# Expert weights in 4 MB loads with 32 KB rows, in a one-core encoder layer with sixteen experts

## The chip, the core and the metric

The kernel runs on one core of one Trainium2 chip. TensorE (PE in the profile) multiplies, VectorE (DVE), ScalarE (ACT) and GpSimd (POOL) do the element work, and sixteen DMA engines move data between HBM and the on-chip memory. SyncE (SP) computes nothing here: its queue issues nearly all loads. The metric is device time in microseconds of one launch. The kernel before took 1243.34 us (median of 3 runs, 1241.81 to 1243.98).

## The reference

```
h   = rmsnorm(x, g_pre_mix) * (1 + scale_m) + shift_m     # x: 512 tokens x 1024
mix = concat(retention(h), dilated_attention(h)) @ w_out
x   = x + gate_m * rmsnorm(mix, g_post_mix)
h   = rmsnorm(x, g_pre_ffn) * (1 + scale_f) + shift_f
aff = softmax(h @ w_router)                               # 16 experts
gates, idx = top_k(aff.T, 64)                             # every expert takes 64 tokens
for e in range(16):
    a = h[idx[e]] @ w_gate[e]                             # (64 x 1024) @ (1024 x 2048)
    u = h[idx[e]] @ w_up[e]
    y = (silu(a) * u) @ w_down[e]                         # (64 x 2048) @ (2048 x 1024)
    moe[idx[e]] += gates[e] * y
x   = x + gate_f * rmsnorm(moe, g_post_ffn)
```

All is float32. Each expert has three weight matrices of 8 MB, so the sixteen experts read 402.7 MB.

## The kernel before

The mixer takes the first 325 us or so and isn't changed but for small things. Then the experts follow one after the other (the loop `for pr in range(E // 2)` takes them in pairs).

**One expert.** `gate_up` computes both first products. The contraction over the 1024 inputs is cut in eight chunks of 128 (K chunks); `chunk_up` takes two of them at a time, loads 256 rows of `w_gate` and 256 of `w_up` (2 MB each), and issues for each weight tile 16 matmuls (L1057): the stationary operand is a 128x64 piece of the gathered tokens (`xeT`), the moving operand 128x512 of weights. Two matmuls stand side by side in the two column halves of the array (`tile_position`, the index `g`). After the eight K chunks the element work and eight transposes (L1074) follow, and `down` (L1099) does the last product with four loads of 512 rows of `w_down` (2 MB each). So an expert consumes twelve 2 MB loads, each with 16 matmuls.

**Rows and K order.** A load gives partition p adjacent rows of the matrix: two rows of 8 KB of `w_gate` or `w_up` (rows 2p and 2p+1 of the 256), four rows of 4 KB of `w_down`. That is 16 KB of adjacent memory per partition. Which input belongs to K chunk k follows from this; `ffn_chunk` (with a step of 2) takes the same inputs out of x for the router's transposes and for the gather.

**Where the weights lie.** Nine tiles of 2 MB are used in turn (`order`): two of `ring_b`, two of `ring_w[0]`, two of `ring_w[1]`, two of `ring_h`, one of `ring_c`. `ring_w` and `ring_h` hold the mixer's split operands before. `wtile` takes the next one and issues its load on SP. SP works in order: a load waits until the matmuls that read the tile's old content are done, and all loads behind it wait too. For the last pair of experts one tile leaves the ring (`own_tile`) and holds rows for the end.

**Work between the matmuls.** PE's order is written out with `pin`. Even experts carry the scatter of the pair before (L1112) between the matmuls of `gate_up`. Odd experts carry the gather for the next pair (L1021: stationary operand a K chunk of x, moving operand a selection matrix) after `gate_up` and between the matmuls of `down`. The last pair carries more: the last selection, sums of rows (L986).

**The end.** After the last expert's `gate_up` the first 512 rows of the result are written by four stores (`out<-w`, L1189, on SP), and at last an indirect store (L1199, on POOL) writes the last expert's 64 tokens over them. It waits for those four stores and for the last row of element work (L1198).

Of the kernel before, what the change touches and what calls it, by code (L numbers as in the profile page):

```python
# [46 lines left out]
def layer(ctx, tc, x, c, w_ada, b_ada, g_pre_mix, g_post_mix, g_pre_ffn, g_post_ffn,  # L47
# [68 lines left out]
    ring_h = pool(ctx, "ring_h", N_R, side="right")  # L116
    hparts_of = [ring_h.tile([P, 2, 4, S], F32R, name="w") for _ in range(2)]
    hhi = [hparts_of[k // 4][:, 0, k % 4] for k in range(KC)]
    hlo = [hparts_of[k // 4][:, 1, k % 4] for k in range(KC)]
# [795 lines left out]
    order = [ring_b] * N_B + [ring_w[0]] * N_R + [ring_w[1]] * N_R + [ring_h] * N_R + [ring_c] * N_C  # L915

    def wtile(shape, src=None):
        t = order[state["n"] % len(order)].tile(shape, F32, name="w")
# [1 line left out]
        if src is not None:  # L920
            nc.sync.dma_start(t, src)
        return t

    def own_tile(shape):

        i = state["n"] % len(order)
        order[:] = order[i:] + order[:i]
        state["n"] = 0
        return order.pop(0).tile(shape, F32, name="w")
# [305 lines left out]
```

## Time and profile before

| what | value |
|---|---|
| median of 3 runs | 1243.34 us |
| the profiled execution's own time | 1243.3 us |
| its span in the trace | 1241.6 us |
| PE busy | 1148.5 us (92%) |
| DVE, ACT, POOL busy | 372.0, 235.5, 83.7 us |
| moved by DMA | 456.02 MB, mean 367 GB/s |
| granted TensorE clock, mean | 0.993 of full |

The span is the trace's first to last event; the execution's own time is 1.7 us longer. Times in rows are microseconds from the span's start. A busy PE is not PE at its peak: matmuls are pipelined, and one that waits for the engine counts as busy.

### The profile page before, as it was taken

How to read it: one execution, taken by the hardware profiler on the slowest of the kernel's cores; microseconds unless marked ns; L12 is line 12 of the kernel's file. 1: busy time of each engine (PE TensorE's matmuls, PEld its weight loads, DVE VectorE, ACT ScalarE, POOL GpSimd, SP SyncE). 2: the span in 40 equal slices, each digit the busy share in tenths (PEclk: the TensorE clock that was granted, in tenths of full speed). 3: DMA queues.
4: the chain of work that ended last, by engine and by line, in shares of the span. 5: the costliest groups of instructions: out<-in, count | busy, mean ns of one | idle time of the engine just before them, and what ended most of it. 6: DMA issues, size and time to landing. Idle time of an engine off the chain costs nothing.

```text
span 1241.6 us, 14130 instructions
## 1 busy us (share of the span) xinstructions
PE 1148.5 (92%) x5756; PEld 546.6 (44%) x5757; DVE 372.0 (30%) x914; ACT 235.5 (19%) x479; POOL 83.7 (7%) x135
## 2 busy tenths in 40 slices
PE   8999999999999999999799879978997898789997
PEld 5777776776443433433243224323332433243332
DVE  4589878666410120121022101200210121012022
ACT  4765335344010100101010101001000100010110
POOL 1622022201000000000000000000000000000012
PEclk8999999999999999999999999999999999999998
DMA  9946745296989999999999999999999999999997
GB/s 292 271 136 196 228 149 146 78 362 252 394 348 427 428 426 427 427 428 425 428 429 425 428 428 427 428 427 427 428 426 428 426 429 426 427 428 427 427 428 309
DMA packets 80520, 456.02 MB, mean 367 GB/s; under 512 B 6180, under 2 KB 41352, under 8 KB 55496
## 3 DMA queue, kind: packets, MB, share of 16 engines
q1 hardware_dynamic: 79384, 450.63, 89.8%
q0 software_dynamic: 656, 2.36, 0.5%
q10 hardware_dynamic: 416, 2.14, 0.4%
q8 instruction: 45, 0.74, 0.2%
q14 instruction: 19, 0.16, 0.0%
HBM read 452.75 MB, written 2.36 MB: 367 GB/s over the span
## 4 chain that ended last, share of the span: by engine, by line
PE 52%; DMA 36%; issue 4%; DVE 4%; ACT 1%; POOL 1%; POOLq 0%; DVEq 0%; SPq 0%; ACTq 0%
PE gu L1057 18%; DMA w<-in_w_up_e 15%; DMA w<-in_w_down_e 15%; PE yb L1099 12%; PE tb L1021 5%; DMA w<-in_w_gate_e 3%; PE pj L104 2%; PE pj L105 2%; PE pj L106 2%; PE sb L1112 2%; DMA wa<-in_w_ada 1%; PE tb L1074 1%; PE at L463 1%; DMA out<-w 1%; PE at L452 1%
## 5 line engine op out<-in xcount | busy, mean ns | idle before, releaser
L1057 PE MATMUL gu<-w,xeT 128*64 128x512 f32 x2032 | 465.9, 600 | 50.9 <-DMA w<-in_w_gate_e 26.2
L1057 PEld LDWEIGHTS gu<-w,xeT 128*64 128x64 f32 x2032 | 135.7, 137 | 336.2 <-issue 244.7
L1099 PE MATMUL yb<-w,wide_h 128*64 128x512 f32 x1024 | 230.0, 596 | 10.5 <-DMA w<-in_w_down_e 10.1
L1099 PEld LDWEIGHTS yb<-w,wide_h 128*64 128x64 f32 x1024 | 70.3, 137 | 144.7 <-issue 126.3
L1071 DVE SCALAR_TENSOR_TENSOR wide_h<-gu,gcol,wide_h 128x512 f32<-128x512 f32 x32 | 24.0, 751 | 294.7 <-PE gu L1057 229.6
L1070 ACT ACTIVATE wide_h<-gu 128x512 f32<-128x512 f32 x32 | 19.1, 597 | 465.1 <-PE gu L1057 413.4
L1127 DVE TENSOR_TENSOR wide_y<-yb,wide_y 64x512 fp32r<-64x512 f32 x30 | 20.7, 689 | 200.0 <-ACT wide_y L1126 200.0
L1021 PE MATMUL tb<-sel,yx 128*128 128x128 f32 x512 | 68.1, 286 | 5.4 <-ACT wide_h L1075 4.7
L1116 DVE TENSOR_TENSOR w<-w,sb 128x512 f32<-128x512 f32 x56 | 38.5, 687 | 112.8 <-PE sb L1112 112.8
L1021 PEld LDWEIGHTS tb<-sel,yx 128*128 128x128 f32 x512 | 62.8, 197 | 21.0 <-ACT xeT L1025 11.4
L1175 POOL TENSOR_TENSOR w<-ident 128x64 f32<-128x64 f32 x2 | 0.6, 318 | 815.6 <-PE gu L1057 815.6
L1126 ACT CAST wide_y<-yb 64x512 fp32r<-64x512 f32 x30 | 17.4, 580 | 186.8 <-PE yb L1099 175.6
L104 PE MATMUL pj<-w,hi 128*128 128x512 f32 x112 | 47.1, 421 | 0.0
L1112 PE MATMUL sb<-wide_y,selT 128*128 128x512 f32 (+1 forms) x128 | 47.1, 448 | 0.0
L318 DVE SCALAR_TENSOR_TENSOR acc<-wa,sc,acc 128x512 f32<-128x512 f32 x56 | 44.4, 792 | 2.8 <-DMA wa<-in_w_ada 2.4
L106 PE MATMUL pj<-w,lo 128*128 128x512 f32 x112 | 44.5, 398 | 0.0
L105 PE MATMUL pj<-w,hi 128*128 128x512 f32 x112 | 44.5, 398 | 0.0
L1027 DVE TENSOR_SCALAR xeT<-tb,mod 128x128 f32<-128x128 f32 x32 | 13.1, 410 | 98.1 <-PE tb L1021 98.1
L1112 PEld LDWEIGHTS sb<-wide_y,selT 128*128 128x128 f32 (+1 forms) x128 | 19.0, 187 | 51.9 <-issue 51.9
L110 DVE TENSOR_TENSOR lo<-w,hi 128x512 fp32r<-128x512 f32 (+1 forms) x52 | 34.9, 674 | 16.0 <-ACT hi L109 11.7
L109 ACT CAST hi<-w 128x512 fp32r<-128x512 f32 (+1 forms) x52 | 30.2, 585 | 49.9 <-PE pj L105 32.1
L442 POOL TENSOR_SCALAR w<-w,rden 128x512 f32<-128x512 f32 x32 | 32.2, 1014 | 110.2 <-DVE rden L441 94.1
(296 smaller groups left out, 1125.4 us busy)
## 6 DMA issues: line engine op xcount, KB each, us to landing
w<-in_w_up_e SPq DMA_DIRECT2D x64, 2048.0 KB, 37.6
w<-in_w_gate_e SPq DMA_DIRECT2D x63, 2048.0 KB
w<-in_w_down_e SPq DMA_DIRECT2D x61, 2048.0 KB, 36.9
wa<-in_w_ada SPq DMA_DIRECT2D x32, 512.0 KB, 4.7
w<-in_w_ada SPq DMA_DIRECT2D x16, 512.0 KB, 7.3
w<-in_w_in SPq DMA_DIRECT2D x14, 512.0 KB, 5.1
w<-in_w_down_e SPq DMA_DIRECT2D x5, 1024.0 KB
w<-in_w_out SPq DMA_DIRECT2D x4, 1024.0 KB
```

Of the source, the lines that this page charges most:

```text
L104: nc.tensor.matmul(o, lhsT=l[0], rhs=r[0], start=start, stop=False)
L105: nc.tensor.matmul(o, lhsT=l[0], rhs=r[1], start=False, stop=False)
L106: nc.tensor.matmul(o, lhsT=l[1], rhs=r[0], start=False, stop=stop)
L109: nc.scalar.copy(hi, src)
L110: nc.vector.tensor_tensor(lo, src, hi, ALU.subtract)
L318: nc.vector.scalar_tensor_tensor(acc, w[:, k], sc[:, 2 * i + k:2 * i + k + 1], acc, ALU.mult, ALU.add)
L442: nc.gpsimd.tensor_scalar(p, p, rden[:, i:i + 1], 1.0, ALU.mult, ALU.mult)
L1021: pin(nc.tensor.matmul(tp[:, j], lhsT=ffn_chunk(x1[:, t], k), rhs=sel[:, t].rearrange("p e c -> p (e c)"), start=(t == 0 and j == 0), stop ...
L1057: pin(nc.tensor.matmul(gu[m][i][64 * g:64 * g + 64], lhsT=xe[:, k], rhs=w[q][:, f:f + 512], start=(k == 0), stop=(k == KC - 1), tile_posit ...
L1099: pin(nc.tensor.matmul(yb[64 * n:64 * n + 64], lhsT=hc(fc), rhs=ws[k][:, 512 * n:512 * n + 512], start=(fc == 0 and seeded is None), stop= ...
L1112: pin(nc.tensor.matmul(sb, lhsT=selT[u, P * t:P * t + P], rhs=y[u, f], start=(i == 0), stop=(i == 1)))
L1116: nc.vector.tensor_tensor(acc_at(t, f), acc_at(t, f), sb, ALU.add)
```

## The change

- From the third expert on the weights come in loads of 4 MB. A partition gets four adjacent rows of `w_gate` or `w_up`, or eight of `w_down`: 32 KB.
- The tiles of the ring are taken as pairs: `ring_b`, `ring_w[0]`, `ring_w[1]`, `ring_h` give four pairs. Three pairs lie side by side in memory and take one 4 MB load each; in the pair `ring_w[0]` the tiles stay apart, and what falls on it comes as two loads of 2 MB. The ninth tile (`own`) leaves the ring with the third expert.
- The first two experts, the last expert's second half of `gate_up` and its `down` keep loads of 2 MB and less. These too follow the new row order.
- The order within `gate_up` becomes: four K chunks of gate, four of up, four of gate, four of up. The step of `ffn_chunk` becomes 4.
- The hidden columns are dealt out otherwise, since partition p now holds rows 8p to 8p+7 of `w_down`: the two matmuls that stand side by side take the even and the odd columns of the weights. Their moving operand is read with a step of two elements (8 bytes) where it was contiguous.
- `wo_parts` and `hparts_of` become one tile each, so that a pair of slots can be taken over as one.

The core of the diff:

```diff
     def ffn_chunk(a, k):
-        return a[..., 256 * (k // 2) + k % 2:256 * (k // 2) + 256:2]
+        return a[..., 512 * (k // 4) + k % 4:512 * (k // 4) + 512:4]
...
-    order = [ring_b] * N_B + [ring_w[0]] * N_R + [ring_w[1]] * N_R + [ring_h] * N_R + [ring_c] * N_C
...
+    pairs = [ring_b, None, *[r.tile([P, 2, 4096], F32, name="w") for r in (ring_w[1], ring_h)]]
+    order = [r if r is None else r[:, i] for r in pairs for i in range(2)] + [own]
...
+    def pair_of(src, rows):
+        n = state["n"] % len(order)
+        if pairs[n // 2] is None:
+            r = rows // 2
+            return [w for h in range(2) for w in units_of(src[:, r * h:r * h + r], r)]
+        state["n"] += 2
+        u = pairs[n // 2].rearrange("p i (s f) -> p (i s) f", s=rows // 2)
+        nc.sync.dma_start(u, src)
+        return [u[:, s] for s in range(rows)]
...
     def rows_up(ex, j):
-        return [wsrc[ex, 256 * j:256 * j + 256].rearrange("(p s) f -> p s f", s=2) for wsrc in (w_gate, w_up)]
+        return [wsrc[ex, 512 * j:512 * j + 512].rearrange("(p s) f -> p s f", s=4) for wsrc in (w_gate, w_up)]
...
-                    f = 1024 * i + 512 * g
-                    pin(nc.tensor.matmul(gu[m][i][64 * g:64 * g + 64], lhsT=xe[:, k], rhs=w[q][:, f:f + 512],
+                    pin(nc.tensor.matmul(gu[m][i][64 * g:64 * g + 64], lhsT=xe[:, k], rhs=w[q][:, 1024 * i + g:1024 * i + 1024:2],
...
     def down_rows(ex, j):
-        return w_down[ex, 512 * j:512 * j + 512].rearrange("(p s) n -> p s n", s=4)
+        return w_down[ex, 1024 * j:1024 * j + 1024].rearrange("(p s) n -> p s n", s=8)
```

Three places of the instruction order. First SP's queue where the third expert's loads begin, before (`w_` and a number is a tile, the brackets say for which engines and DMA lanes the load waits):

```order
139 L921 DMA w_3729<-in_w_gate_e 128x4096 [waits DMAHW2_49,PE_49]
140 L921 DMA w_3731<-in_w_up_e 128x4096 [waits DMAHW3_49,PE_49]
141 L921 DMA w_3757<-in_w_gate_e 128x4096 [waits DMAHW4_49,PE_49]
142 L921 DMA w_3759<-in_w_up_e 128x4096 [waits DMAHW5_49,PE_49]
143 L921 DMA w_3793<-in_w_gate_e 128x4096 [waits DMAHW6_49,PE_49]
144 L921 DMA w_3795<-in_w_up_e 128x4096 [waits DMAHW7_49,PE_49]
145 L921 DMA w_3839<-in_w_gate_e 128x4096 [waits DMAHW0_49,PE_49]
```

and the same place after the change (`w_3293` is the pair of `ring_w[1]`, `w_3294` that of `ring_h`):

```order
139 L941 DMA w_3293<-in_w_gate_e 128x8192 [waits DMAHW2_49,PE_49]
140 L941 DMA w_3294<-in_w_up_e 128x8192 [waits DMAHW4_49,DMAHW3_49,PE_49]
141 L941 DMA ring_b_2763<-in_w_gate_e 128x8192 [waits DMAHW7_49,DMAHW6_49,PE_49]
142 L930 DMA w_3818<-in_w_up_e 128x4096 [waits DMAHW5_49,DMAHW0_49,PE_49]
143 L930 DMA w_3820<-in_w_up_e 128x4096 [waits DMAHW1_49,PE_49]
```

These five loads bring the whole of the expert's `gate_up`, for which eight loads stood (seven are shown). A load into a pair waits for the matmuls of both tiles' old contents. The fifth load of before went to the ninth tile; now the third load goes on to `ring_b`.

Second the first loads into the mixer's old tiles, before and then after:

```order
119 L921 DMA w_3365<-in_w_gate_e 128x4096 [waits PE_49]
120 L921 DMA w_3367<-in_w_up_e 128x4096 [waits PE_49]
121 L921 DMA w_3405<-in_w_gate_e 128x4096 [waits PE_49]
122 L921 DMA w_3407<-in_w_up_e 128x4096 [waits PE_49]
123 L921 DMA w_3436<-in_w_up_e 128x4096 [waits DMAHW0_49]
```

```order
119 L930 DMA w_3367<-in_w_gate_e 128x4096 [waits PE_49]
120 L930 DMA w_3386<-in_w_up_e 128x4096 [waits PE_49]
121 L930 DMA w_3293<-in_w_gate_e 128x4096 [waits PE_49]
122 L930 DMA w_3293<-in_w_up_e 128x4096
123 L930 DMA w_3294<-in_w_up_e 128x4096 [waits DMAHW0_49]
```

Rows 121 and 122 went to two tiles, each with its own wait for PE; now they are the halves of one tile, and the first of them has the only wait.

Third PE's queue in the third expert's `gate_up`, the first matmuls, before and then after (`gu` is the product in PSUM, `sb` the scatter):

```order
1467 L1057 MATMUL gu_3725<-w,xeT 64x512 [waits DMAHW2_49]
1468 L1057 MATMUL gu_3725<-w,xeT 64x512
1469 L1057 MATMUL gu_3726<-w,xeT 64x512 x2
1470 L1057 MATMUL gu_3725<-w,xeT 64x512 x2
1471 L1057 MATMUL gu_3726<-w,xeT 64x512 x2
1472 L1057 MATMUL gu_3727<-w,xeT 64x512 [waits DMAHW3_49]
```

```order
1468 L1086 MATMUL gu_3713<-w,xeT 64x512 [waits DMAHW2_49]
1469 L1086 MATMUL gu_3713<-w,xeT 64x512
1470 L1086 MATMUL gu_3714<-w,xeT 64x512 x2
1471 L1086 MATMUL gu_3713<-w,xeT 64x512 x2
1472 L1086 MATMUL gu_3714<-w,xeT 64x512 x2
1473 L1086 MATMUL gu_3713<-w,xeT 64x512 x2
1474 L1086 MATMUL gu_3714<-w,xeT 64x512 x2
1475 L1142 MATMUL sb<-wide_y,selT 128x512 [waits Activation_49]
1476 L1142 MATMUL sb<-wide_y,selT 128x512 [waits DVE_49]
```

One row stands for a side-by-side pair or two. The wait for the next load came after 16 matmuls of 2 MB and now comes after 32 of 4 MB.

## Rows read from the trace of the kernel before

**Rows 1.** The page: GB/s in 40 equal slices of the span.

```profile
GB/s 292 271 136 196 228 149 146 78 362 252 394 348 427 428 426 427 427 428 425 428 429 425 428 428 427 428 427 427 428 426 428 426 429 426 427 428 427 427 428 309
```

**Rows 2.** Two pairs of experts: stretch, busy by engine, clock, DMA share, GB/s.

```profile
425.00:528.00 103.00, 101.76 (x494) 40.00 (x492) 16.64 (x40) 9.27 (x17) 0.00 (x0) 1.00 1.01 427
620.00:738.00 118.00, 105.35 (x498) 39.71 (x494) 16.61 (x40) 9.87 (x18) 0.00 (x0) 1.00 1.01 427
```

**Rows 3.** PE in order of time, end of the fourteenth expert's `gate_up`: start, duration, [idle before].

```profile
1088.45 3.65 PE L1057 MATMUL gu<-w,xeT 128*64 128x512 f32 x16 [1.25 <-DMA w<-in_w_gate_e]
1093.34 3.65 PE L1057 MATMUL gu<-w,xeT 128*64 128x512 f32 x16 [1.24 <-DMA w<-in_w_up_e]
...
1153.20 3.65 PE L1057 MATMUL gu<-w,xeT 128*64 128x512 f32 x16 [0.30 <-DMA w<-in_w_up_e]
```

**Rows 4.** Weight loads of PE in order of time, last expert's `down`.

```profile
1228.55 0.14 PEld L1099 LDWEIGHTS yb<-w,wide_h 128*64 128x64 f32 x2 [0.29 <-issue]
1229.27 0.28 PEld L1099 LDWEIGHTS yb<-w,wide_h 128*64 128x64 f32 x4 [0.58 <-DMA w<-in_w_down_e]
...
1231.80 0.32 PEld L1099 LDWEIGHTS yb<-w,wide_h 128*64 128x64 f32 x4 [0.54 <-DMA w<-in_w_down_e]
```

**Rows 5.** DVE's last instruction; then the last store in the chain of waits.

```profile
1235.19 0.75 DVE L1198 SCALAR_TENSOR_TENSOR w<-w,sf 128x512 f32<-128x512 f32 x1 [0.66 <-POOL sf L1197]
...
1224.33 12.35 DMA out<-w
```

**Rows 6.** DMA queue q1 in three stretches (600:1200, 1226:1231, 3:8): packets, MB, share.

```profile
DMA packets 17593, 256.27 MB, mean 427 GB/s; under 512 B 1950, under 2 KB 1950, under 8 KB 1950
q1 hardware_dynamic: 17569, 255.91, 100.4%
...
DMA packets 467, 1.88 MB, mean 377 GB/s; under 512 B 54, under 2 KB 54, under 8 KB 420
q1 hardware_dynamic: 467, 1.88, 92.4%
...
q1 hardware_dynamic: 491, 1.82, 96.0%
```

**Rows 7.** SP's queue in order of time, loads of the first three experts.

```profile
297.19 0.33 SPq L921 DMA_DIRECT2D w<-in_w_gate_e  x1
303.02 0.81 SPq L921 DMA_DIRECT2D w<-in_w_up_e  x2
...
370.35 0.33 SPq L921 DMA_DIRECT2D w<-in_w_gate_e  x1
...
401.25 0.33 SPq L921 DMA_DIRECT2D w<-in_w_up_e  x1
...
422.02 0.33 SPq L921 DMA_DIRECT2D w<-in_w_gate_e  x1
```

**Rows 8.** DMA share (last but one) and GB/s; then tenths busy in 40 slices of 294:299.

```profile
368.00:371.00 3.00, 3.00 (x17) 1.00 (x14) 0.00 (x0) 0.00 (x0) 0.00 (x0) 1.00 0.15 60
...
DMA  9988420010000000000000000000000009930356
```

**Rows 9.** Groups of PE (count, busy us, mean ns, idle before) and of its weight loads.

```profile
L1057 PE MATMUL gu<-w,xeT 128*64 128x512 f32 x2032 | 465.9, 600 | 50.9 <-DMA w<-in_w_gate_e 26.2 <-DMA w<-in_w_up_e 24.2 <-DVE xeT L1027 0.5
...
L1099 PE MATMUL yb<-w,wide_h 128*64 128x512 f32 x1024 | 230.0, 596 | 10.5 <-DMA w<-in_w_down_e 10.1
...
L1021 PEld LDWEIGHTS tb<-sel,yx 128*128 128x128 f32 x512 | 62.8, 197 | 21.0 <-ACT xeT L1025 11.4 <-ACT wide_h L1075 6.1 <-issue 2.4
L1074 PEld LDWEIGHTS tb<-ident,wide_h 128*128 128x128 f32 x128 | 17.9, 208 | 20.3 <-DVE wide_h L1071 14.1 <-ACT wide_h L1075 6.2
L1112 PEld LDWEIGHTS sb<-wide_y,selT 128*128 128x128 f32 x112 | 16.7, 188 | 45.4 <-issue 45.4
...
L807 PEld LDWEIGHTS at<-ident,yx 128*128 128x128 f32 x32 | 4.6, 207 | 2.8 <-issue 1.6 <-PE m L106 0.9
L950 PEld LDWEIGHTS tb<-ident,sel 128*128 128x128 f32 x32 | 3.8, 144 | 0.0
```

More of the change, by code (lines that the diff above doesn't have):

```diff
@@ L115, in layer @@
     sm = pool(cm, "sm", 4)
[L116 to L119, printed above, removed]
+    ring_h = pool(ctx, "ring_h", side="right")
+    hparts_of = ring_h.tile([P, 2, 2, 4, S], F32R, name="w")
+    hhi = [hparts_of[:, k // 4, 0, k % 4] for k in range(KC)]
+    hlo = [hparts_of[:, k // 4, 1, k % 4] for k in range(KC)]
     wsp = pool(cq, "wsp", 2, side="right")
@@ L684, in layer @@
     cq.close()
-    ring_w = [pool(ctx, f"ring_w{n}", N_R, side="right") for n in range(2)]
+    ring_w = [pool(ctx, f"ring_w{n}", 2 - n, side="right") for n in range(2)]
+    wo_parts = ring_w[1].tile([P, 2, 2, 4, 512], F32R, name="w")
     KS = [4, 5, 6, 7, 0, 1, 2, 3]
@@ L696, in wo_split @@
         yield
-        parts = ring_w[n].tile([P, 2, 4, 512], F32R, name="w")
+        parts = wo_parts[:, i] if n else ring_w[0].tile([P, 2, 4, 512], F32R, name="w")
         hi, lo = parts[:, 0], parts[:, 1]
@@ L910, in layer @@
     mw = pool(ctx, "mw", 1)
-    ring_c = pool(ctx, "ring_c", N_C)
+    own = pool(ctx, "own").tile([P, 4096], F32, name="own")
     psg = pool(ctx, "psg", 1, space=PSUM)
@@ L914, in layer, with unit, units_of, large @@
     state = {"n": 0}
[L915 to L918 removed]
+    pairs = [ring_b, None, *[r.tile([P, 2, 4096], F32, name="w") for r in (ring_w[1], ring_h)]]
+    order = [r if r is None else r[:, i] for r in pairs for i in range(2)] + [own]
+    def unit():
         state["n"] += 1
[L920 to L929, printed above, removed]
+        o = order[(state["n"] - 1) % len(order)]
+        return ring_w[0].tile([P, 4096], F32, name="w") if o is None else o
+    def units_of(src, rows, cut=None):
+        u = unit().rearrange("p (s f) -> p s f", s=rows)
+        for s0, m in cut or ((0, rows),):
+            nc.sync.dma_start(u[:, s0:s0 + m], src[:, s0:s0 + m])
+        return [u[:, s] for s in range(rows)]
[7 more added lines that the diff above has]
+        nc.sync.dma_start(u, src)
+        return [u[:, s] for s in range(rows)]
+    def large(ex, late):
+        if ex < WHOLE:
+            return False
+        if len(order) % 2:
+            while state["n"] % len(order) % 2:
+                state["n"] += 1
+            if state["n"] % len(order) == len(order) - 1:
+                state["n"] += 1
+            state["n"] %= len(order)
+            order.pop()
+        return ex < E - 1 or not late
     def acc_tiles():
@@ new lines, in down @@
+        for j in range(2):
+            src = down_rows(ex, j)
+            whole = large(ex, True)
+            if whole:
+                ws = pair_of(src, 8)
+            for h in range(2):
+                if whole:
+                    w = ws[4 * h:4 * h + 4]
+                elif first and (j, h) == (0, 0):
+                    w = [first[s // 2][:, s % 2] for s in range(4)]
+                else:
+                    w = units_of(src[:, 4 * h:4 * h + 4], 4, None if ex < E - 1 or j == 0 else ((0, 2), (2, 1), (3, 1)) if h else ((0, 2), (2, 2)))
+                for s in range(4):
+                    fc = 8 * j + 4 * h + s
+                    for n in range(2):
+                        pin(nc.tensor.matmul(yb[64 * n:64 * n + 64], lhsT=hc(fc), rhs=w[s][:, 512 * n:512 * n + 512],
+                           start=(fc == 0 and seeded is None), stop=(fc == 15), tile_position=(0, 64 * n)))
+                    if s % 2:
+                        next(side, None)
@@ L1143, in layer @@
         sels = pair_sel(es, gcol)
-        if last:
-            own = own_tile([P, 4096])
         if pr == 0:
```

69 lines of the change are left out of this document (28 added, 41 removed).

## Prediction

> **What bounds the kernel now.** I read the GB/s line of the page first. From the thirteenth slice (372 us) to the last but one it stands at 425 to 429 [rows 1]: the stream of weights never pauses there. Then two pairs of experts by stretch. Between 425 and 528 us a pair takes 103 us with PE busy all along; between 620 and 738 us it takes 118 us, PE is busy for 105, DMA for all of it [rows 2]. So PE starts behind a full ring, empties it, and from about 570 us waits for weights. In such a stretch a burst of 16 matmuls starts at each landing, 4.89 us apart (1088.45, 1093.34), works 3.65 us and waits 1.25 [rows 3]. A load of 2.097 MB in 4.9 us is the 427 GB/s again.
>
> The end is less plain. The wait at 1093.34 (the fourteenth expert's last weights) is PE's last long one: the scatter, the last selection and the sums of rows then keep it busy, and up to 1233 us it waits for weights only 0.30 us at 1153.20 [rows 3] and twice in the last `down`, 0.58 and 0.54 where 0.29 is usual between weight loads, so 0.29 and 0.25 [rows 4]. From 1093 us on PE's own work and the stream are level. The last row of element work is ready at 1235.19 + 0.75 = 1235.94; the last plain store lands at 1224.33 + 12.35 = 1236.68 and releases the indirect store [rows 5]. The stream wins by 0.7 us. A change must therefore be followed on two paths: the stream, and PE from the fourteenth expert's last weights on.
>
> **Part 1: longer rows (gain).** Does a longer packet cost less per byte? Between 600 and 1200 us queue q1 moved 17569 packets, 1950 of them under 512 B; the other 15619 share 255.91 MB, 16 KB each [rows 6]. The engines' time is 1.004 x 16 x 600 us, or 617.1 ns a packet. At 1226 to 1231 us there are 366 packets of 4 KB and 47 of 8 KB (467 less 54 small ones; 420 under 8 KB) in 0.924 x 16 x 5 = 73.9 us [rows 6]. If a packet costs a + b per KB, then a + 16b = 617.1 and 413a + 1840b = 73920, hence a = 9.9 ns. The stretch 3 to 8 us gives another end: 1.82 MB of 4 KB packets in 0.960 x 80 us are 173 ns each [rows 6], hence a = 25 ns; those loads start into an empty queue, so I take 10, the row on the saturated queue. No row shows a packet above 16 KB. If it stays cut at 16 KB the gain is nothing; that is the other end of the range.
>
> A 4 MB load has 128 rows, 8 per engine; each saves one a, 80 ns per load. The order has 60 such loads: 80 pairs of 2 MB from the third expert to the last one's first half, less the quarter that falls on `ring_w[0]`. All 60 make 4.8 us. Up to the fourteenth expert's last weights, and after the gap below, there are 51: -4.1 us.
>
> **Part 2: a pair must be free as a whole (loss, once).** While PE leads, a load leaves when PE frees its tile. The load at 370.35 finds the stream empty (DMA share 0.15 between 368 and 371) [rows 7, 8]; bytes follow an issue by about 0.9 us (issue at 297.19; the DMA line of 294 to 299 fills at its 34th of 40 slices, 298.1) [rows 7, 8]. So the stream restarts at about 371.2. Ten loads leave between 370.35 and 401.25, 49.0 us of work at 4.9: it lasts to 420.2. Before, two more loads had left by then. Now the third 4 MB load needs both tiles of `ring_b`, and the second of these is freed at 422.02 [rows 7]; its bytes come at 423.0. The gap is 423.0 - 420.2 = 2.8 us; since the restart is only known to half a us, I take +2.5. All weights behind it are that much later. The first loads into `ring_w[1]` leave at 303.02 instead of 297.19 [rows 7], since both halves of `wo_parts` must be read out. That lateness of 5.8 us meets the idle 368 to 371.2 and, what is left, the gap just counted; it isn't added. After 423 I see no second gap: the three pairs besides the one in use are 12 MB, 29 us of stream, in which PE would have to free nothing.
>
> **Part 3: PE gets 4 MB at once (loss at the end).** In the middle it costs nothing: PE has 15 us to spare per pair of experts [rows 2]. But an odd expert's last weights are a 4 MB load now. After its landing PE has 32 matmuls left instead of 16: 3.65 us more at the most [rows 3], and I take 3.4, since a burst right behind another one has its fill hidden. In the fourteenth expert this starts the tail: +3.4 us.
>
> **Sum.** PE's path at the end: -4.1 + 2.5 + 3.4 = +1.8. The waits in it vanish, as the stream is 2 us ahead: -0.30 - 0.29 - 0.25 = -0.8. That leaves +1.0. The stream's path ends at +2.5 - 4.8 = -2.3, so now PE's row decides instead of the store, and the 0.7 us by which the store was later are won: +0.3. The profiled execution took 1243.3 us (1.7 outside its span of 1241.6), as good as the median of 1243.34. Forecast: 1243.6 us.
>
> **Edits I cost at nothing.** Two more small transposes in `ffn_cols`, another layout of the router's weights, four steps of `chunk_up` instead of eight: all under the mixer or the stream. The ninth tile's loss is in part 2. The moving operand's step of 8 bytes: no row has such a read in float32. Weight loads of 128 columns do: 197 ns with a step of 8 bytes (L1021) against 188 contiguous (L1112), and 207 against 144 among transposes (L807, L950) [rows 9]. These bound it at 0, +5% and +44%. I take 0: weight loads with a step of 16 bytes (L1074, 208 ns) cost what those with 8 do (L807, 207) [rows 9], so it isn't the step's width that sets the pace there; and where a pair of matmuls has 0.46 us for 512 columns (3.65 / 8), a weight load reads its 128 in 0.2.
>
> **Rivals.**
> - *A packet's fixed price is 25 ns.* Part 1 becomes -10.2, PE's path 1.0 - 6.1 = -5.1, the end -5.8: 1237.5 us. For it: the first stretch of rows 6. Against it: that queue was starting.
> - *The rows are cut at 16 KB.* No gain: the path is +5.1, the end +4.4: 1247.7 us. For it: nothing longer than 16 KB in the trace; against it: two rows of 8 KB travel as one packet of 16 today.
> - *The moving operand's step slows PE (slower).* It counts where PE leads: in the first two experts, whose frees set part 2, and in the last two. Four times 465.9 / 16 = 29.1 us [rows 9], so 1.2 us per per cent; from 2% on the run is measurably slower. At 5% it is 5.8 us: 1249.4 us. At 44% PE bounds everything: 16 x 12.8 = 205 us more, less the waits of 50.9 + 10.5 [rows 9]: about 1387 us. Against it: the weight loads just named.
> - *The gather's stationary step of 16 bytes (8 before) doubles its weight load.* 128 loads by 197 ns in the two gathers before 422 us, 64 in the tail: +25 +13, 1281 us. Against it: 208 and 207 ns [rows 9].
> - *The gap of part 2 or the lateness of part 3 doesn't come,* because a tile is free earlier or the fourteenth expert has time after all: 2.5 to 3.4 less, about 1240.5 us.
>
> [...]
>
> **How the numbers follow.** Forecast 46% (its own range 1241 to 1246), dear packets 17, cut rows 12, slow moving reads 13, slow gather 3, no gap 9. Three runs spread over 0.17%, so 0.2% (2.5 us) is about what can be told from no change: 1240.8 and 1245.8 are the borders. Faster: 15 of the second, 6 of the last, 5 of the forecast: 0.26. Slower: 11 of cut rows, 12 and 3 of the slow reads, 3 of the forecast: 0.29. The same: 0.45. The range reaches to the dear packets and past the cut rows: 1238.0 to 1248.5.
>
> **What would show it.** Part 1: above 427 GB/s between 600 and 1080 us, near 431, and fewer packets per MB (32 KB ones). Part 2: a dent in the stream at 421 to 423 us. Part 3: bursts of 32 matmuls of about 7.1 us with waits near 2.7, no wait of PE for weights behind the fourteenth expert's `gate_up`, and the indirect store released by DVE's last row. L1057's mean (600 ns) and L1021's weight load (197 ns) should stay. A slower `gate_up` while PE leads, or a stream still at 427, would prove me wrong.

## The result, and the profile after

The changed kernel takes 1271.74 us (median of 6 runs, 1269.83 to 1272.95) against 1243.38 us before (6 runs): ratio 1.0228, 95% interval 1.0214 to 1.0241, 28.4 us slower. The forecast was 1243.6 us. The profiled execution has a span of 1270.2 us, 28.6 more than before.

First the page: busy time of the engines, GB/s in 40 slices, and the chain of waits by engine.

```profile
PE 1221.1 (96%) x5759; PEld 604.7 (48%) x5759; DVE 372.2 (29%) x914; ACT 235.7 (19%) x479; POOL 83.9 (7%) x135
...
GB/s 287 279 133 216 224 131 122 106 337 266 405 286 432 273 434 430 429 426 432 431 429 429 426 433 431 431 431 425 426 435 429 429 414 425 435 428 431 426 424 146
...
PE 72%; DMA 14%; issue 6%; DVE 5%; ACT 1%; POOL 1%; SPq 0%; POOLq 0%; DVEq 0%; ACTq 0%
```

PE was busy for 1148.5 us and had 52% of the chain; now it is 1221.1 us and 72%. The stream, level at 425 to 429 in [rows 1], now runs at about 430, with a hole in the fourteenth slice (273). Which operations hold the added 72.6 us? The largest groups (count, busy us, mean ns, idle before), to be laid beside [rows 9]:

```profile
L1086 PE MATMUL gu<-w,xeT 128*64 128x512 f32 x1520 | 361.1, 619 | 16.0 <-DMA w<-in_w_up_e 11.2
L1086 PE MATMUL gu<-ring_b,xeT 128*64 128x512 f32 x496 | 118.3, 616 | 0.5 <-DVE xeT L1053 0.5
L1129 PE MATMUL yb<-w,wide_h 128*64 128x512 f32 x736 | 162.1, 594 | 0.0
L1129 PE MATMUL yb<-ring_b,wide_h 128*64 128x512 f32 x272 | 67.3, 632 | 0.0
L1047 PE MATMUL tb<-sel,yx 128*128 128x128 f32 x512 | 127.5, 404 | 5.4 <-ACT wide_h L1104 4.7
L1047 PEld LDWEIGHTS tb<-sel,yx 128*128 128x128 f32 x512 | 121.9, 328 | 21.3 <-ACT xeT L1051 8.1
```

The gather's weight load (L1021 before, L1047 now) takes 328 ns instead of 197; `gate_up` (L1057, now L1086) has a mean of 619 and 616 instead of 600; `down` (L1099, now L1129) is nearly as before, 229.4 us in its two groups against 230.0. Now single runs of matmuls in order of time (start, duration): 16 of the same gather and the last 32 of the last `gate_up`, first before the change, then after it:

```profile
412.30 2.15 PE L1021 MATMUL tb<-sel,yx 128*128 128x128 f32 x16
...
1209.74 7.04 PE L1057 MATMUL gu<-w,xeT 128*64 128x512 f32 x32
```

```profile
425.68 4.00 PE L1047 MATMUL tb<-sel,yx 128*128 128x128 f32 x16
...
1239.30 7.38 PE L1086 MATMUL gu<-w,xeT 128*64 128x512 f32 x32
```

16 gather matmuls cost 1.85 us more, the 64 of a pair 7.4, the 512 of the kernel 59. The 32 matmuls of `gate_up` took 7.04 us and take 7.38, so +5%, some 1.4 us per expert and 22 in all; and they start 29.6 us later. (Groups of PE overlap at their edges: the `gate_up` matmuls that start at 1108.92 below take 7.65 us, and the transposes behind them start at 1116.50. So these two, 81 us together, needn't add up to 72.6.) Now a stretch of [rows 2], and the hole (busy by engine, clock, DMA share, GB/s):

```profile
620.00:738.00 118.00, 113.44 (x496) 47.12 (x494) 16.61 (x40) 9.28 (x17) 0.00 (x0) 0.99 1.00 430
429.00:440.50 11.50, 11.50 (x51) 6.56 (x53) 2.60 (x10) 0.92 (x2) 0.00 (x0) 1.00 0.14 40
```

In the hole PE is busy all along and DMA is not: 11.5 x (1 - 40 / 430) = 10.4 us of stream are lost. SP's queue says why; its rows answer to [rows 7]:

```profile
410.77 0.33 SPq L941 DMA_DIRECT2D w<-in_w_up_e  x1
439.10 0.33 SPq L941 DMA_DIRECT2D ring_b<-in_w_gate_e  x1
```

Before, the second tile of `ring_b` got its 2 MB load at 422.02 (by the prediction's reading of [rows 7]); the 4 MB load that needs both tiles leaves at 439.10 now: the gather stands among the `down` matmuls that free `ring_b`.

Where the 28.6 us come from is seen stretch by stretch, first before, then after:

```profile
290.00:425.00 135.00, 131.18 (x717) 62.52 (x717) 39.74 (x135) 18.45 (x43) 2.75 (x5) 1.00 0.94 384
425.00:545.00 120.00, 118.76 (x566) 45.44 (x562) 20.09 (x45) 10.42 (x19) 0.00 (x0) 1.00 1.01 427
```

```profile
290.00:425.00 135.00, 131.17 (x641) 65.85 (x631) 37.00 (x123) 17.55 (x41) 3.11 (x7) 1.00 0.87 358
425.00:545.00 120.00, 117.97 (x518) 51.25 (x516) 17.05 (x41) 9.74 (x18) 0.00 (x0) 1.00 0.91 389
545.00:665.00 120.00, 115.44 (x502) 48.60 (x498) 16.60 (x40) 9.28 (x17) 0.00 (x0) 0.99 1.01 431
```

At 427 GB/s the stream loses (384 - 358) x 135 / 427 = 8.2 us and (427 - 389) x 120 / 427 = 10.7, together 18.9, all of it before 545 us. From there it runs full and PE waits for it again, so slow reads cost nothing more in the middle; but a stream that runs full makes nothing good either, except by its longer rows. The end of the fourteenth expert's `gate_up`, where the transposes start, before and then after:

```profile
1096.92 0.75 PE L1074 MATMUL tb<-ident,wide_h 128*128 128x128 f32 x4
```

```profile
1108.92 7.65 PE L1086 MATMUL gu<-w,xeT 128*64 128x512 f32 x32 [1.28 <-DMA w<-in_w_up_e]
1116.50 0.75 PE L1103 MATMUL tb<-ident,wide_h 128*128 128x128 f32 x4
```

The changed kernel is 19.6 us late there: the 18.9, less some 4 by the longer rows (an estimate from part 1's figures below: 71 us over 16 engines in 600 us), and 4.0 since 7.65 us of matmuls instead of 3.65 [rows 3] follow the last landing. Behind it, where PE sets the pace, 9.0 more come, 7.4 of them from the gather's 64 matmuls.

### The profile page after: what moved, and what is told of

It reads as the page before. It is cut to its first block, busy times and chain, and to the rows that moved or that the text cites. A ratio compares the mean times of both kernels' runs of the same rounds, so it can differ in the third digit from the quotient of the medians.

```text
span 1270.2 us, 14007 instructions
## 1 busy us (share of the span) xinstructions
PE 1221.1 (96%) x5759; PEld 604.7 (48%) x5759; DVE 372.2 (29%) x914; ACT 235.7 (19%) x479; POOL 83.9 (7%) x135
## 4 chain that ended last, share of the span: by engine, by line
PE 72%; DMA 14%; issue 6%; DVE 5%; ACT 1%; POOL 1%; SPq 0%; POOLq 0%; DVEq 0%; ACTq 0%
PE gu L1086 27%; PE yb L1129 17%; DMA w<-in_w_up_e 12%; PE tb L1047 10%; PE sb L1142 3%; DMA wa<-in_w_ada 2%; PE tb L1103 2%; PE pj L105 2%; PE pj L107 1%; PE pj L106 1%; DVE acc L319 1%; PE at L464 1%; PE at L453 1%; PE m L884 1%; PE tb L986 1%
## 5 line engine op out<-in xcount | busy, mean ns | idle before, releaser
L1086 PE MATMUL gu<-w,xeT 128*64 128x512 f32 x1520 | 361.1, 619 | 16.0 <-DMA w<-in_w_up_e 11.2
L1086 PEld LDWEIGHTS gu<-w,xeT 128*64 128x64 f32 x1520 | 100.8, 135 | 240.3 <-issue 214.8
L1129 PE MATMUL yb<-w,wide_h 128*64 128x512 f32 x736 | 162.1, 594 | 0.0
L1047 PE MATMUL tb<-sel,yx 128*128 128x128 f32 x512 | 127.5, 404 | 5.4 <-ACT wide_h L1104 4.7
L1047 PEld LDWEIGHTS tb<-sel,yx 128*128 128x128 f32 x512 | 121.9, 328 | 21.3 <-ACT xeT L1051 8.1
L1086 PE MATMUL gu<-ring_b,xeT 128*64 128x512 f32 x496 | 118.3, 616 | 0.5 <-DVE xeT L1053 0.5
L1099 ACT ACTIVATE wide_h<-gu 128x512 f32<-128x512 f32 x32 | 19.1, 598 | 442.3 <-PE gu L1086 326.4
L1129 PEld LDWEIGHTS yb<-w,wide_h 128*64 128x64 f32 x736 | 51.8, 137 | 100.1 <-issue 99.2
L1129 PE MATMUL yb<-ring_b,wide_h 128*64 128x512 f32 x272 | 67.3, 632 | 0.0
L1086 PEld LDWEIGHTS gu<-ring_b,xeT 128*64 128x64 f32 x496 | 33.0, 134 | 70.2 <-issue 69.4
## 6 DMA issues: line engine op xcount, KB each, us to landing
w<-in_w_down_e SPq DMA_DIRECT2D x15, 2048.0 KB, 28.6
```

The lines of the kernel that those rows point to most:

```text
L1047: pin(nc.tensor.matmul(tp[:, j], lhsT=ffn_chunk(x1[:, t], k), rhs=sel[:, t].rearrange("p e c -> p (e c)"), start=(t == 0 and j == 0), stop ...
L1129: pin(nc.tensor.matmul(yb[64 * n:64 * n + 64], lhsT=hc(fc), rhs=w[s][:, 512 * n:512 * n + 512], start=(fc == 0 and seeded is None), stop=( ...
```

## The experiments

Four theories were tested. A: the gather's read with a step of 16 bytes is the main loss. B: the moving operand's step of 8 bytes is. C: the pairs of slots are. And, once the loss was settled, J: the rest of the change would win, but for TensorE's last wait for 4 MB.

**Each read put back.** The first edit is `e1_gather2`, the second `e2_rhs1`, both together `e3_both`. Of each matmul only the changed argument is shown. In these kernels, and in e4, e5, e6, e8, e9 and e10 below, inputs no longer meet their own weights: they give times, not the layer's result.

```diff
-lhsT=ffn_chunk(x1[:, t], k), rhs=sel
+lhsT=x1[:, t, 256 * (k // 2) + k % 2:256 * (k // 2) + 256:2], rhs=sel
```

```diff
-rhs=w[q][:, 1024 * i + g:1024 * i + 1024:2]
+rhs=w[q][:, 1024 * i + 512 * g:1024 * i + 512 * g + 512]
```

> The changed kernel, with one slice put back: the gather's weight loads (tb) read every second word of x1 instead of every fourth, so its K chunks hold other inputs than the weights that they meet. Theory A (the gather's 16-byte step is the main loss): weight loads of the gather back from 328 to about 197 ns and 16 matmuls from 3.93 to about 2.08 us, so 512 of them give back some 59 us of PE, which falls from 1221 to about 1162 us; the loads bound again and the time is 1245 to 1251 us, since the gate and up matmuls stay at 28.9 us per 128. Rival B (the moving operand's 8-byte step is the main loss): the gather was never what delayed the frees, and the time stays above 1262 us. Rival C (pairs of slots that must be free as a whole are the loss): above 1262 us too, with the idle stretch of the DMA at 429 to 440 us as long as now (10.8 us lost).

> The changed kernel, with the moving operand of the gate and up matmuls read as 512 adjacent words instead of every second one (columns of the FFN are then in another order than the rows of w_down that they meet). Theory A: 128 of these matmuls go from 28.86 back to 27.47 us, PE falls by 32 x 0.69 = 22 us to about 1199 us, but the gather stays at 3.93 us per 16, the DMA still idles some 9 to 11 us near 430 us, and the time is 1252 to 1264 us. Rival B: 1243 to 1250 us. Rival C: 1262 us or more.

> The changed kernel with both reads put back (gather at every second word, moving operand adjacent): what is left is the 4 MB loads, the pairs of slots and the order of K. Theory A, the forecast's own sum: 1243.6 us, PE busy about 1140 to 1150 us; with what the trace after shows of stretches in which the DMA idles at 294 to 304 and 376 to 380 us (6 and 3.5 us more than before) it could be up to 1249 us. Rival C (pairs cost by themselves): 1255 us or more.

Measured, beside 1243.31 us for the kernel before: e1 1247.09 us (ratio 1.0035, 1.0024 to 1.0047), e2 1265.18 (1.0182, 1.0165 to 1.0199), e3 1242.71 (0.9996, 0.9985 to 1.0007). The gather's step alone gives back 24.6 of 28.4 us, the moving operand's alone 6.6, both together 29.0, and nothing is left over. e2 is 1 us above what A expected, where C allowed it; but e1 and e3 lie far under what C asked for (1262 and 1255 us or more), and e1 and e2 against B. The weight loads of e1 and the same stretch of e3 (PE busy first):

```profile
L1047 PEld LDWEIGHTS tb<-sel,yx 128*128 128x128 f32 x512 | 62.9, 197 | 21.1 <-ACT xeT L1051 11.4
```

```profile
620.00:738.00 118.00, 105.50 (x494) 40.84 (x492) 16.61 (x40) 9.28 (x17) 0.00 (x0) 0.97 1.01 431
```

197 ns are back, and in e3 PE's need per pair (105.35 in [rows 2]) too, at 431 instead of 427 GB/s.

**The price by step.** `e4_steps`:

```diff
+GS = [4, 1, 2, 3, 4, 5, 6, 8]
...
-lhsT=ffn_chunk(x1[:, t], k), rhs=sel
+lhsT=x1[:, t, k:k + 127 * GS[es[0] // 2] + 1:GS[es[0] // 2]], rhs=sel
...
-rhs=w[q][:, 1024 * i + g:1024 * i + 1024:2]
+rhs=w[q][:, i + g:i + g + 511 * (1 + ex % 4) + 1:1 + ex % 4]
```

> The changed kernel with reads of several steps in one run, inputs not matched to weights: the gather of pair 0 to 7 reads x1 at a step of 4, 1, 2, 3, 4, 5, 6, 8 words, and gate and up read their moving operand at a step of 1, 2, 3, 4 words in expert 0, 1, 2, 3 and again from there. If what counts is how many of a read's words share 16 bytes (theory A), the gather's weight load takes about 190 ns at step 1, 197 at 2, something between at 3, 328 at 4, and still 328 at 5, 6 and 8; the matmuls at 3 and 4 cost more than the +5% at step 2. If the span of the read counts (rival D), the weight load goes on growing: 5, 6 and 8 take some 400, 470 and 600 ns. If 2 is as good as 1 for a moving operand and the +5% has another cause (rival E), step 1 and 2 take the same 28.9 us per 128. The time by itself says nothing here.

Gather rows of the pairs whose step is 1, 2, 3, 4, 5, 6 and 8 words (16 matmuls each):

```profile
421.10 2.05 PE L1048 MATMUL tb<-sel,yx 128*128 128x128 f32 x16
...
569.88 2.15 PE L1048 MATMUL tb<-sel,yx 128*128 128x128 f32 x16
...
678.40 3.04 PE L1048 MATMUL tb<-sel,yx 128*128 128x128 f32 x16
...
832.85 4.00 PE L1048 MATMUL tb<-sel,yx 128*128 128x128 f32 x16
...
946.54 3.79 PE L1048 MATMUL tb<-sel,yx 128*128 128x128 f32 x16
...
1102.10 3.82 PE L1048 MATMUL tb<-sel,yx 128*128 128x128 f32 x16
...
1216.24 4.10 PE L1048 MATMUL tb<-sel,yx 128*128 128x128 f32 x16
```

And `gate_up`, its moving operand at a step of 1, 2, 3 and 4 words (32 matmuls each):

```profile
614.50 7.09 PE L1087 MATMUL gu<-w,xeT 128*64 128x512 f32 x32
637.71 7.39 PE L1087 MATMUL gu<-ring_b,xeT 128*64 128x512 f32 x32
...
736.56 11.05 PE L1087 MATMUL gu<-w,xeT 128*64 128x512 f32 x32
763.73 14.56 PE L1087 MATMUL gu<-ring_b,xeT 128*64 128x512 f32 x32
```

The price rises from 2 words to 4 and stays near there up to 8 (3.79 to 4.10 us): rival D (the span of the read) falls, and so does E (the +5% comes with the step of 2). What theory A counts here, the words of a read that share 16 bytes, fits both columns: as a stationary operand 2.05 us at a step of 1 word, 2.15 at 2, 3.04 at 3 and 3.79 to 4.10 from 4 on, as a moving one 7.09, 7.39, 11.05 and 14.56. All of these reads are float32, and no run tries another type. Two words in 16 bytes are not quite free: they cost 4% as a moving operand (7.39 to 7.09) and 5% as a stationary one (2.15 to 2.05).

**The same reads without pairs of slots.** `e5_before_gather4` and `e6_before_rhs2` put one read each into the kernel before; `e7_no_large` is the changed kernel with 2 MB loads alone; its ring has eight tiles, as the ninth still leaves with the third expert.

```diff
-lhsT=ffn_chunk(x1[:, t], k), rhs=sel
+lhsT=x1[:, t, 512 * (k // 4) + k % 4:512 * (k // 4) + 512:4], rhs=sel
```

```diff
-rhs=w[q][:, f:f + 512],
+rhs=w[q][:, 1024 * i + g:1024 * i + 1024:2],
```

```diff
-        return ex < E - 1 or not late
+        return False
```

> The kernel before, with one slice changed: the gather's weight loads read every fourth word of x1 (its K chunks then hold other inputs than the weights that they meet). Weight loads 328 instead of 197 ns, PE +59 us to about 1208 us. Theory A (a slow gather costs by itself, since a pair of experts then needs some 113 of the 118 us in which its weights arrive and the time lost in the first pairs isn't made good): 1255 to 1268 us, near the 1265.2 us of the changed kernel with only the gather slow. Rival C (the pairs of slots, which must be free as a whole, turn the late PE into lost DMA time): without pairs the loads go on while the gather runs, and the time stays at 1243 to 1250 us.

> The kernel before, with the moving operand of gate and up read at every second word (columns in another order than the rows of w_down that they meet). 128 of these matmuls 28.9 instead of 27.5 us, PE +22 us to about 1171 us. In the changed kernel with a fast gather the same step cost 1247.1 - 1242.7 = 4.4 us. Theory A: the same here, 1245 to 1249 us. Rival C: half of it or less, 1243 to 1245 us, as a slot here is 2 MB and comes free by itself.

> The changed kernel without its 4 MB loads: all loads stay at 2 MB, with 16 KB of adjacent rows, and each slot of 2 MB is waited for by itself; order of K, columns and both steps as in the changed kernel. Theory A (the reads on PE are the loss, the loads are not): 1262 to 1274 us, no idle stretch of the DMA of over 8 us at 425 to 445 us but later waits in its place. Rival C (pairs of slots): 1255 us or less.

Measured beside 1242.28: e5 1256.44 (1.0109, 1.0091 to 1.0126), e6 1243.69 (1.0010, 1.0000 to 1.0019), e7 1266.11 (1.0192, 1.0174 to 1.0210). The gather costs 14.2 us here and 22.5 in the changed kernel (e2 less e3), the moving operand 1.4 and 4.4 (e1 less e3). e5 and e7 lie where A put them, e6 where C did: a late PE is dearer in the changed kernel. Whether its pairs or its ring of eight tiles make it so is not told apart. Together the reads cost 23.8 us without any 4 MB load, more than 14.2 + 1.4. The surplus isn't lost in the middle: there PE has 4 us to spare per pair in e5 and 1 in e7, and the stream runs full in both. First e5, then e7:

```profile
425.00:545.00 120.00, 118.76 (x534) 55.00 (x535) 17.61 (x44) 9.86 (x19) 0.00 (x0) 1.00 1.00 425
620.00:738.00 118.00, 113.75 (x512) 48.47 (x510) 16.60 (x40) 9.27 (x17) 0.00 (x0) 1.00 1.01 427
...
412.82 0.33 SPq L921 DMA_DIRECT2D w<-in_w_gate_e  x1
430.03 0.33 SPq L921 DMA_DIRECT2D w<-in_w_up_e  x1
```

```profile
425.00:545.00 120.00, 118.76 (x522) 51.64 (x518) 17.04 (x41) 9.74 (x18) 0.00 (x0) 1.00 0.96 404
620.00:738.00 118.00, 116.76 (x516) 48.30 (x514) 16.60 (x40) 9.27 (x17) 0.00 (x0) 1.00 1.01 427
...
410.69 0.33 SPq L930 DMA_DIRECT2D w<-in_w_up_e  x1
431.51 0.33 SPq L930 DMA_DIRECT2D ring_b<-in_w_gate_e  x1
```

It is lost early: 404 against 425 GB/s over 120 us are 5.9 us. One reason stands in SP's rows: the load that leaves at 412.82 in e5 goes to the ninth tile. e7 has none, and behind 410.69 its next load waits for `ring_b` until 431.51; a 2 MB load is 4.9 us of stream. No run has both slow reads and nine tiles, so how much of the surplus is the ring's isn't shown.

**Versions with short steps.** `m1_mended` stores x1 in K's order, reads w_down as two times 16 KB and gives the moving operand adjacent words as e2 does; in `m3_pairs8`, shown against m1, VectorE moves pairs of words. Both compute the whole layer. The core of the edits:

```diff
+    def x1_chunk(t, k):
...
+        return x1[:, t, P * k:P * k + P]
...
+    def by_chunk(a):
...
+        return a.rearrange("p (s q) -> p s q", s=4)
...
+    def in_rows(a):
...
+        return a.rearrange("p (q s) -> p s q", s=4)
...
-        nc.vector.tensor_tensor(x1[:, t, g], b, GM[:, g], ALU.mult)
+        nc.vector.tensor_tensor(by_chunk(x1[:, t, g]), in_rows(b), in_rows(GM[:, g]), ALU.mult)
...
+        return w_down[ex, 1024 * j:1024 * j + 1024].rearrange("(h p s) n -> p h s n", h=2, s=4)
```

```diff
-        return x1[:, t, P * k:P * k + P]
+        return x1[:, t, 256 * (k // 2) + k % 2:256 * (k // 2) + 256:2]
...
-        return a.rearrange("p (s q) -> p s q", s=4)
+        return a.rearrange("p (a q b) -> p a q b", a=2, b=2)
```

> A version that keeps the 4 MB loads and gives PE adjacent words in both places: x1 is stored with its columns in the order of K (512 j + 4 q + s stands at 512 j + 128 s + q; VectorE writes and reads it so), the moving operand of gate and up is adjacent, and w_down's 4 MB come as two times 16 KB of adjacent rows per partition. Weight loads of the gather about 190 ns, spacing 112 ns, PE some 3 us under the 1156.8 us of the changed kernel with both reads put back. Theory A: the loads bound it; 1242.7 us of that kernel, plus 0 to 2 us for 16 KB instead of 32 KB packets in a third of the bytes: 1241 to 1246 us, no real difference to the kernel before. Rival F: VectorE's 16-byte reads and writes of x1 in the 16 operations before the routing cost 0.5 us or more each on the path: 1247 to 1255 us.

> The mended version, with x1 stored so that VectorE moves pairs of adjacent words (8 bytes at every 16) and the gather reads every second word: d = 512 j + 4 q + 2 a + b stands at 512 j + 256 a + 2 q + b. In the mended version before this VectorE's 8 products m x GM took 1065 instead of 690 ns and its 8 residual sums 1132 instead of 748 ns, and the first load behind the routing was issued 3.7 us later after the same start. Theory F2 (two words in 16 bytes are enough for VectorE too): 690 to 800 ns each, and 1241.5 to 1245 us. Rival: an 8-byte piece costs VectorE as much as a 4-byte one, 1050 ns or more, and 1246 to 1249 us.

Measured: m1 1246.56 us (1.0037, 1.0023 to 1.0051), a little above theory A and near rival F; m3 1245.04 (1.0014, 1.0005 to 1.0023), at the upper edge of F2. VectorE in m1, then in m3 (mean ns behind the busy time):

```profile
L813 DVE SCALAR_TENSOR_TENSOR yx<-yx,v,xr 128x512 f32<-128x512 f32 x8 | 8.7, 1132 | 1.4 <-POOL v L811 1.4
...
L805 DVE TENSOR_TENSOR yx<-m,GM 128x512 f32<-128x512 f32 x8 | 8.5, 1063 | 7.8 <-ACT junk L789 7.6
```

```profile
L822 DVE SCALAR_TENSOR_TENSOR yx<-yx,v,xr 128x512 f32<-128x512 f32 x8 | 5.7, 748 | 1.5 <-POOL v L819 1.4
L813 DVE TENSOR_TENSOR yx<-m,GM 128x512 f32<-128x512 f32 x8 | 5.5, 686 | 8.1 <-ACT junk L797 8.0
```

Adjacent words took 748 and 688 ns (the same rows of the changed kernel). Single words at every 16 bytes cost VectorE half as much again (1132 and 1063 ns); pairs of words cost nothing (748 and 686): F2 holds. m3 stays 2.3 us above e3, and the two intervals just touch. It has 2560 more packets (128 for each of 20 loads); 20 loads by 80 ns, the prediction's price, would be 1.6 of it. That is an estimate, and the rest isn't explained.

**The wait for the output projection's weights.** In e3 the first load into `ring_w[1]` leaves at 300.9 us, not at 297.19 [rows 7]. `e8_wo_apart` (on e3) and `m4_wo_apart` (on m3) make it two tiles again:

```diff
-        parts = wo_parts[:, i] if n else ring_w[0].tile([P, 2, 4, 512], F32R, name="w")
+        parts = ring_w[n].tile([P, 2, 4, 512], F32R, name="w")
...
-        if pairs[n // 2] is None:
+        if pairs[n // 2] in ring_w:
```

> The changed kernel with both reads put back (inputs not matched to weights, as there), and with ring_w[1] as two tiles of 2 MB again: the output projection's weights lie in two tiles, the first of which comes free earlier, and expert weights go there in 2 MB loads. In the kernel with both reads put back the DMA lost 9.7 us at 292 to 302 us, against 3.55 us before the change, as the first load into ring_w[1] was issued at 300.9 us and not at 297.2. Theory G (that wait is a price of the change which the forecast had not named, and which hid its gain): the loss falls to 4 to 6 us, against it a quarter of the 4 MB loads come in 16 KB packets again (about 1.3 of the 5 us that the larger packets give), so the time goes from 1242.7 to 1237 to 1241 us, faster than the kernel before. Rival H (idle time so early is made good later in any case): 1242 to 1245 us.

> The mended version with pairs of words, and ring_w[1] as two tiles of 2 MB again: all that computes is as the reference asks. Theories F2 and G together: 1237 to 1241.5 us, faster than the kernel before by 0.1 to 0.5%. If G falls (rival H): 1242 to 1246 us.

Measured: e8 1245.98 (1.0025, 1.0013 to 1.0038), m4 1247.62 (1.0040, 1.0027 to 1.0053). Theory G falls. In e8 that load leaves at 295.90, yet between 290 and 425 us the stream reaches 378 GB/s against 376 in e3, with PE busy for 131.2 of the 135 us in both: PE's frees bound it there, as part 2 said ("isn't added"). And both got slower than the kernels they come from, 1.0 and 1.6 us above rival H's range too. The last long waits of PE for weights, in e3 and then in e8:

```profile
1079.54 16.80 PE L1086 MATMUL gu<-w,xeT 128*64 128x512 f32 x64 [5.56 <-DMA w<-in_w_gate_e]
```

```profile
1091.63 9.68 PE L1085 MATMUL gu<-w,xeT 128*64 128x512 f32 x32 [6.07 <-DMA w<-in_w_up_e]
```

e3 ends these matmuls at 1096.3 us, e8 at 1101.3. With another count of slots in pairs, the wait for 4 MB fell on the up weights, with a whole 4 MB of work behind it, and the clock fell there (0.50 from 1091.6 to 1096.0 us): 9.68 us for 32 matmuls. That made theory J. The clock of e3 in that place (last but two):

```profile
1079.50:1084.00 4.50, 4.46 (x12) 1.38 (x14) 0.00 (x0) 0.00 (x0) 0.00 (x0) 0.50 1.03 444
```

**The last experts in 2 MB loads.** `e9_last_small` (on e3), `m5_last_small` (on m4) and `m6_last_small` (on m3):

```diff
-        return ex < E - 1 or not late
+        return ex < E - 2
```

> The changed kernel with both reads put back (inputs not matched to weights, as there), whose last two experts get their weights in 2 MB loads. With 4 MB loads TensorE waited 5.56 us for the fifteenth expert's second gate weights, ran the next 64 matmuls in 16.80 us instead of 14.1 at a granted clock of 0.50 at first, and ended at 1096.3 us; from there to its end it waits for no weights. Theory J (the 4 MB grain and the clock behind it set the end): with 2 MB it ends 3.65 us behind the landing of the last up weights at about 1089.5 us, near 1093 us, and the time goes from 1242.7 to 1239 to 1240.5 us. Rival K (the end is set by the last loads of w_down, not by these matmuls): 1242 to 1243.5 us.

> The mended version with pairs of words and ring_w[1] as two tiles, the last two experts' weights in 2 MB loads. There TensorE waited 6.08 us for the fifteenth expert's second up weights (4 MB) and ran 32 matmuls in 8.67 us. Theory J: 16 matmuls less behind the last landing (3.5 us) and no fall of the clock (1.6 us): 1247.6 goes to 1241.5 to 1243 us. Rival K: 1246 to 1248 us.

> The mended version with pairs of words and ring_w[1] as one tile, the last two experts' weights in 2 MB loads. Theory J: 1245.0 goes to 1241 to 1242.5 us, 0.1% under the kernel before. Rival K: 1244 to 1246 us.

Measured beside 1243.18: e9 1243.81 (1.0000, 0.9991 to 1.0010), m5 1247.16 (1.0035, 1.0021 to 1.0048), m6 1244.49 (1.0009, 1.0000 to 1.0018), as rival K says (e9 0.3 us above its range). But the edit had missed: the waits in question belong to the fourteenth expert, not to the fifteenth as I had written, and stood there as before (5.57 us in e9, 6.08 in m5). One expert earlier, `e10_last3_small`, `m7_last3_small` and `m8_last3_small`:

```diff
-        return ex < E - 1 or not late
+        return ex < E - 3
```

> The changed kernel with both reads put back (inputs not matched to weights, as there), whose last three experts get their weights in 2 MB loads. With 4 MB loads TensorE waited 5.56 us for the fourteenth expert's second gate weights, ran the next 64 matmuls in 16.80 us instead of 14.1 at a granted clock of 0.50 at first, and ended at 1096.3 us; from there on it waits for weights 0.4 us in all. Theory J (4 MB at once and the clock behind it set the end): it ends 3.65 us behind the landing of the last up weights at about 1089.5 us, near 1093 us, and the time goes from 1242.7 to 1239 to 1241 us, under the kernel before. Rival K (the end is set by something else, as the last loads of w_down): 1242 to 1244 us.

> The mended version with pairs of words and ring_w[1] as two tiles, the last three experts' weights in 2 MB loads. There TensorE waited 6.08 us for the fourteenth expert's second up weights and ran 32 matmuls in 8.67 us. Theory J: 16 matmuls less behind that landing (3.5 us) and no fall of the clock (1.6 us): 1247.6 goes to 1241.5 to 1243 us. Rival K: 1246 to 1248 us.

> The mended version with pairs of words and ring_w[1] as one tile, the last three experts' weights in 2 MB loads. Theory J: 1245.0 goes to 1241 to 1242.5 us, 0.1% under the kernel before. Rival K: 1244 to 1246 us.

Measured beside 1243.34: e10 1241.82 (0.9989, 0.9980 to 0.9998), m7 1245.17 (1.0015, 1.0007 to 1.0024), m8 1243.67 (1.0006, 0.9997 to 1.0015). The last wait of e10:

```profile
1090.72 3.65 PE L1086 MATMUL gu<-w,xeT 128*64 128x512 f32 x16 [1.25 <-DMA w<-in_w_up_e]
```

It ends at 1094.4, and the 16 matmuls took 3.65 us, as before the change [rows 3]. The times fall by 0.9, 2.45 and 1.4 us, a quarter to a half of what J expected, and all three lie between J's range and K's. The intervals of m4 and m7 don't overlap, so J's direction is shown there; e3 with e10 and m3 with m8 alone wouldn't show it. The shorter work behind the last landing and the time of a matmul there change together (16 in 3.65 us in e10, 64 in 16.80 in e3), so which of them gives the gain isn't told apart. e10 is the only kernel faster than the one before, by 0.1%, and it matches no inputs to weights; of the versions that do, m8 comes to the time of before and none beats it.

## Why the prediction was wrong

**The step that failed** is among the edits costed at nothing: "weight loads with a step of 16 bytes (L1074, 208 ns) cost what those with 8 do (L807, 207), so it isn't the step's width that sets the pace there". Both rows are transposes. For the gather's matmuls the step does set the pace, 328 ns against 197, and that term, put at 0, took 24.6 of the 28.4 us. The change moved the router's transposes from 8 to 16 bytes too, and they stayed at 207 ns (L807 before, now L809):

```profile
L809 PEld LDWEIGHTS at<-ident,yx 128*128 128x128 f32 x32 | 4.6, 207 | 2.8 <-issue 2.5
```

So the rows were read rightly and say nothing of matmuls; why transposes don't pay was not tested. The moving operand's step was put at 0 by the same rows and by how fast a weight load reads; it cost 5%, 4.4 to 6.6 us here. The nearer row was L1021 itself: an ordinary matmul's load that already paid 5% for 8 bytes (197 against 188 on L1112).

**The fourth rival** (3 in 100, 1281 us) named the cause, a slow weight load of the gather, and the places too: it counted the 128 matmuls of the first two gathers and the 64 in the tail, and held the middle to be free. The middle was free: from 545 to 1145 us the stream ran at 426 to 431 GB/s. What was wrong is its price of 197 ns a load: no run shows a load that doubles; it grew by 131 ns, the spacing by 1.85 us / 16 = 115. At 115 ns its sum is 14.7 + 7.4 = 22.1 us, and the gather alone cost 22.5 (e2 less e3). So close a fit is partly luck, as the same matmuls cost 14.2 in the kernel before (e5).

**The third rival** (the moving operand, 13 in 100) had the right size as well: +5% at 5.8 us, measured 4.4 (e1 less e3) with a fast gather, 6.6 with the slow one and 1.4 in the kernel before.

**Part 1** holds. Between 600 and 1200 us, against [rows 6]:

```profile
DMA packets 11077, 257.14 MB, mean 429 GB/s; under 512 B 1224, under 2 KB 1224, under 8 KB 1224
...
q1 hardware_dynamic: 11053, 256.77, 100.0%
```

9829 packets share about 256.8 MB, so some 5800 are of 32 KB and 4000 of 16. A MB took 1.004 x 9600 / 255.91 = 37.66 us of an engine and takes 37.39; over 256.77 MB that is 71 us, or 12 ns per 32 KB packet, give or take 2 for the rounded shares. The forecast took 10.

**Part 2** has its dent in e3, where nothing else is slow: 186 of 431 GB/s for 3 us, so 1.7 us lost, against 2.5.

```profile
418.50:421.50 3.00, 3.00 (x18) 1.00 (x16) 0.00 (x1) 0.00 (x0) 0.00 (x0) 1.00 0.64 186
```

In the changed kernel it is 10.4 us. That is mostly the gather's doing: with its read put back (e1) the stream runs at 431 GB/s from 425 to 545 us.

**Part 3** was put at 3.4 us; taking it away gave 0.9 to 2.5. The forecast did not have the clock's fall behind the wait of 5.56 us for 4 MB: in e3 the granted clock was 0.50 for 4.5 us there, and 64 matmuls took 16.80 us, where twice 7.04 would be 14.1. (PE's room per pair was 12.65 us by [rows 2], 118 less 105.35, not 15; nothing hung on it.)

**The sum** of the three parts, +0.3 us, was right for the kernel it described: e3 came out at -0.6 (-1.9 to +0.9). That interval is wider than the errors of the single terms, so it doesn't test them. A range that ended at 1248.5 left out the fourth rival, and the only rows against that one were of transposes.

## What to carry to other kernels

When a layout changes, list every read whose step changes, on each engine, and price it on a row of the same instruction kind: a transpose is no stand-in for a matmul's weight load (207 ns at both steps here, against 197 and 328). Where K's order has to follow the weights' rows, keep at least two adjacent words of the activations together; here that cost VectorE nothing (686 against 688 ns) and the gather 5% (2.15 against 2.05 us). And look for a loss where the slower engine leads: here the slow reads cost nothing while PE waited for a full stream, and all that was lost in the first two gathers, and again in the tail, stood in the time.

## What the runs showed of the hardware that I had not expected

Matmuls that read float32 at a step of 3 words took 1.5 times as long as with adjacent words in the stationary operand (3.04 to 2.05 us) and 1.56 times in the moving one (11.05 to 7.09); at 4 words it is 1.95 and 2.05 times, and up to 8 words the stationary one stays at 1.85 to 2.0. VectorE's product on 512 words goes from 688 to 1063 ns at single words 16 bytes apart and stays at 686 with pairs. Behind a wait of 5.6 us (e3) and 6.1 us (e8) for a 4 MB load the granted clock of PE was 0.50, over 4.5 and 4.4 us; behind the 1.25 us waits for 2 MB loads in e10 16 matmuls took their 3.65 us. Shorter waits were followed by a fall too: in the kernel before the clock was 0.57 from 617 to 621 us, behind a wait of 2.46 us. The same time of 8.78 us that 32 matmuls took there stands behind 2.19 us in e3:

```profile
1050.40 8.78 PE L1129 MATMUL yb<-w,wide_h 128*64 128x512 f32 x32 [2.19 <-DMA w<-in_w_down_e]
```

In e9 32 matmuls behind waits of 2.22 and 2.55 us took 7.09. The kernels with 4 MB loads and fast reads show a mean granted clock of about 0.98 (0.975 to 0.988 by run), the runs of the one before 0.993 to 0.999.
